# Two modulations' sums in another stage, and fewer steps and an earlier state in the state-space stage

## The chip, the cores and the metric

The kernel runs on one core of a Trainium2 chip. The metric is the device time of one execution in microseconds. The engines are TensorE (PE: matmuls; PEld: its weight loads), VectorE (DVE), ScalarE (ACT), GpSimd (POOL) and SyncE (SP), which issues nearly all transfers.

## The reference, cut to what matters

A block with attention and convolution and a gated feed-forward part come first; then a state-space mixer, then a mixer with stick-breaking attention. All in float32, 512 positions, width 1024.

```python
def swiglu_ffn(h, w_ffn_in, w_ffn_out):          # D_FF = 2816
    g, u = jnp.split(h @ w_ffn_in, 2, axis=-1)
    return (jax.nn.silu(g) * u) @ w_ffn_out

# state-space mixer: 32 heads of 64 in 4 groups, state of 128, chunks of 128 positions
z, xbc, dt = split(h @ in_w)
xbc = silu(causal_dwconv(xbc, conv_w, conv_b))   # -> xs, bm, cm
def step(state, inp):                            # one chunk
    acum = jnp.cumsum(ac, axis=1)
    seg = jnp.where(causal, acum[:, :, None] - acum[:, None, :], -jnp.inf)
    scores = einsum('btgn,bsgn->btsg', cc, bc)[..., None] * jnp.exp(seg)
    y_diag = einsum('btsgh,bsghp->btghp', scores, xc)
    y_off = einsum('btgn,bghpn->btghp', cc, state) * jnp.exp(acum)[..., None]
    new_state = state * jnp.exp(acum[:, -1]) + einsum('bsgn,bsghp->bghpn', bc, xc * w_end)
    return new_state, y_diag + y_off
y = (y + d_skip * xs) * silu(z);  y = group_rmsnorm(y) * norm_g;  x = x + gate * (y @ out_w)

# modulations: shift, scale, gate of each stage
shift, scale, gate = split(silu(c) @ ada_w[i] + ada_b[i], 3)     # ada_w[i]: 1024 x 3072
```

The modulation that the change speaks of is the shift and the scale of the last stage (`ada_w[1]`, columns 0 to 2047).

## The kernel before

**Products.** A float32 product is made of three matmuls: each operand is split in a high part (`fp32r`) and the rest. `mm3` issues high x high, L328, and the two mixed ones, L329 and L330. The stages run one after the other; each overlaps its edges with the next.

**Weights.** Each stage has a plan, a list of weight units of 512 KB in the order of their use. `load` (L247) brings a unit into one of four raw buffers (`NRAW`), `split` makes the high half `whi` on ACT (L269) and the low half `wlo` on DVE (L273), in a ring of four (`NRING`); PE frees a ring slot when it is done with the unit.

**Sums.** A modulation is a product of one row with a 1024 x 1024 matrix. It is not done on PE: eight loads of 512 KB go through the same raw buffers, and DVE adds each, times its scalar, to an accumulator `acc` (L503 the first, L505 the others). `add` puts the sums in the plan, `self.rate` of them after each weight unit. Sixteen steps after the eighth sum, `fin` adds up the partitions with 32 tiny matmuls (L487) and DVE turns the result into columns (L526 and L527 for a scale, such as `Gk`; L524 for a shift, such as `Sk`). While `summing` is set, the next modulation's first sum isn't started, and nothing behind it in the plan is:

```python
n = self.rate                                                # add()
self.plan += self.sums[:n]
if isinstance(u, Sums) and u.k == 0 and self.summing:        # advance()
    return False
```

**Steps.** The program text is a list of small steps. `run` merges lists by their share done (a list of 10 beside a list of 100 has one step for each ten) and after each step `pump` moves the plan on. The merged order, and a table of priorities by name (`PRIO`), give each instruction its place; a scheduler then fixes one order for each engine. Each engine executes its list in that order.

**Feed-forward stage** (about 320 to 650 us). `main` projects 256 columns of the gate and 256 of the other half in turn; ACT evicts the gate with SiLU (L1098), DVE multiplies (L1104) into `b` tiles. `Out` then projects back; its operands are split by L90 (ACT) and L91 (DVE).

**State-space stage** (about 690 to 1050 us). The input projection goes group by group; the projection of group g+1 (`main[g + 1]`) is merged with the steps `s` and `e` of `ssd(g)`; the last group is merged with the last z tiles (four products of 512 columns, evicted by ACT with SiLU, L1131) and the first output steps. In a group of eight heads:
- `scores`: four matmuls (L1234) and a copy on ACT (L1236). `bt`: transposes B (L1245), splits B (L1247) and C.
- `decay(i)`, for each of 8 heads: POOL masks (L1263), ACT takes four exponentials (L1266), DVE multiplies by the scores (L1268).
- `xs(c)`, for each of 4 chunks: PE transposes (L1275), DVE scales twice (L1277, L1278), POOL makes `xw` (L1282), ACT and POOL split it (L1239, L1240).
- `diag(c)`: 16 small matmuls (L1292); the first of a group waits for all eight decays. `state(c)`, c = 0 to 2: three matmuls, then a copy (L1315) or an addition on DVE (L1319), and the split again (L1239, L1240). `off(c)`, c = 1 to 3: three matmuls that read the split state of c-1.
- `e`: `gate`, `factor`, `norm` (L1338) and `trans` (L1344, copy L1345), which give the output projection's operand.

The accumulators in PSUM are of two kinds of four: `pa` for projections and `ps` for the rest.

Of the kernel before, what the change touches and what calls it, by code (L numbers as in the profile page):

```python
# [18 lines left out]
D = 1024  # L19
NT = S // P  # L20
# [109 lines left out]
class Body:  # L130
# [934 lines left out]
    def ffn(self):  # L1065
        nc, A = self.nc, self.A
        w = A["w_ffn_in"][0]
        a2, kw = A["ada_w_2"], A["kv_ada_w_2"]
        F = 2816
        g, gt, box = [], {}, {}  # L1070
        act = lambda: self.h

        def egt(t, ps):
            gt[t] = self.w512()
            nc.scalar.activation(gt[t], ps, AF.Silu)

        def eut(t, ps):
            nc.vector.tensor_tensor(gt[t], ps, gt[t], ALU.mult)
            pt = self.psum()
            for j in range(4):  # L1080
                nc.tensor.transpose(pt[:, j * P : (j + 1) * P], gt[t][:, j * P : (j + 1) * P], self.ident)
            nc.scalar.copy(g[0][:, :, t * P : (t + 1) * P], pt.rearrange("p (j c) -> p j c", j=4))


        self.first["ffn"] = self.proj_t(w, 0, act, egt, first=True)
        self.sums = (self.ada_row(A["ada_w"][0], 5 * D, A["ada_b"][:, 5 * D : 6 * D], A["ffn_post_g"], self.c1, "g2")
                     + self.ada_cols(a2[0], D, self.c2, "bGm", "gGm", "Gm")
                     + self.ada_cols(a2[0], 0, self.c2, "bSm", None, "Sm")
                     + self.ada_cols(kw, D, self.c2, "bGk", "gGk", "Gk")
                     + self.ada_cols(kw, 0, self.c2, "bSk", None, "Sk"))  # L1090
        ut = self.proj_t(w, F, act, eut)
        main = []
        for u0 in range(512, F, 256):
            gs = {}

            def eg(j, ps, gs=gs):
                gs[j] = self.w512()
                nc.scalar.activation(gs[j], ps, AF.Silu)  # L1098

            def eu(j, ps, gs=gs, u0=u0):  # L1100
                i = u0 // P + j
                if i // 4 == len(g):
                    g.append(self.big())
                nc.vector.tensor_tensor(g[i // 4][:, i % 4, :], ps, gs[j], ALU.mult)  # L1104

            main += self.proj_f(w, u0, 256, act, eg) + self.proj_f(w, F + u0, 256, act, eu)
        out = Out(self, A["w_ffn_out"][0], list(range(F // P)), lambda k: g[k // 4][:, k % 4, :])
        assert not self.sums
        yield
        self.stage = "ffn"  # L1110
        g.append(self.big())
        self.run(ut)
        self.run(main)
        self.run(out.rest(0))
        self.h = self.new_h()
        self.boundary(out, lambda: self.mods["g2"], True, ("Gm", "Sm"), act, self.first["mamba"])

    def mamba(self):
        nc, A = self.nc, self.A
# [33 lines left out]
        def pxbc(g):  # L1153
            return (self.proj_f(w, 4096 + g * P, P, act, conv(16 + g, lambda j: BC[0][:, 2 * (g % 2), :]))
                    + self.proj_f(w, 4608 + g * P, P, act, conv(20 + g, lambda j: BC[0][:, 2 * (g % 2) + 1, :]))
                    + self.proj_f(w, 2048 + g * 512, 512, act, conv(4 * g, dst(g))))
# [4 lines left out]
        def edt(ps):  # L1161
# [7 lines left out]

        pdt, dt1 = self.proj_32(w, 5120, act, lambda: self.dt_bias, edt)  # L1170
        a2 = A["ada_w_2"]
        self.sums = (self.ada_row(a2[0], 2 * D, A["ada_b_2"][0:1, 2 * D :], None, self.c2, "gm")
                     + self.ada_cols(a2[1], D, self.c2, "bGs", "gGs", "Gs")
                     + self.ada_cols(a2[1], 0, self.c2, "bSs", None, "Ss"))
        main = [pxbc(0)]
        for g in range(1, 4):
            main.append((self.proj_t(w, (g - 1) * 512, act, ez(g - 1)) if g > 1 else []) + pxbc(g))
# [45 lines left out]
        def ssd(g):  # L1223
# [121 lines left out]
                nc.scalar.copy(yT[g][:, :, cs_[c]], ps.rearrange("p (j c) -> p j c", j=4))  # L1345

            L = lambda f, *a: self.at(f.__name__, [lambda: f(*a)])[0]
            s = [L(rows, 0), L(rows, 1), L(scores), L(bt), L(xs, 0)] + [L(decay, i) for i in range(8)]
            s.insert(-2, L(state, 0))
            for c in range(NT):  # L1350
                if c + 1 < NT:
                    s += [L(xs, c + 1)]
                s += [L(diag, c)]
                if c > 0:
                    s += [L(off, c)]
                if 0 < c < NT - 1:
                    s += [L(state, c)]
            e = [L(gate, c) for c in range(NT)] + [L(factor), L(norm, 0)]
            for c in range(NT):
                e += ([L(norm, c + 1)] if c + 1 < NT else []) + [L(trans, c)]  # L1360
            return s, e
# [1 line left out]
        for g in range(3):  # L1363
            s, e = ssd(g)
            self.run(main[g + 1], s + e)
        s, e = ssd(3)
        self.run(main[4], s)
        self.run(out.steps((0, 1), range(4)), e)
# [357 lines left out]
```

## Time and profile before

| | |
|---|---|
| median of 3 runs | 1396.39 us (1393.24 to 1396.82) |
| profiled execution | 1390.66 us, span 1388.9 us |
| granted clock of TensorE, mean | 0.987 |
| PE busy | 1315.3 us (95%) |
| DVE, ACT, POOL busy | 885.8, 665.0, 313.8 us |

Busy time is a mean over stages with different limits; the state of one stage is read from a stretch of the trace. In a timeline's row the bracket is the time that the engine was idle before the instruction and what ended it. The time of the profiled execution lies 1.8 us over its span.

### The profile page before, as it was taken

How to read it: one execution, taken by the hardware profiler on the slowest of the kernel's cores; microseconds unless marked ns; L12 is line 12 of the kernel's file. 1: busy time of each engine (PE TensorE's matmuls, PEld its weight loads, DVE VectorE, ACT ScalarE, POOL GpSimd, SP SyncE). 2: the span in 40 equal slices, each digit the busy share in tenths (PEclk: the TensorE clock that was granted, in tenths of full speed). 3: DMA queues.
4: the chain of work that ended last, by engine and by line, in shares of the span. 5: the costliest groups of instructions: out<-in, count | busy, mean ns of one | idle time of the engine just before them, and what ended most of it. 6: DMA issues, size and time to landing. Idle time of an engine off the chain costs nothing. (4 is left out here: it accounts for less than half of the span.)

```text
span 1388.9 us, 19707 instructions
## 1 busy us (share of the span) xinstructions
PE 1315.3 (95%) x7477; PEld 1026.1 (74%) x7479; DVE 885.8 (64%) x1268; ACT 665.0 (48%) x1216; POOL 313.8 (23%) x321
## 2 busy tenths in 40 slices
PE   7799789999999999999999999999899999999997
PEld 5583566777888888888768777778688787777766
DVE  7844864466355443622768889767744966777865
ACT  5422375355222223412667566667542835555543
POOL 3441322014000000000111434342400412333421
PEclk9999989999999999999999999999999999999999
DMA  9679544205466655223157445424024354232311
GB/s 299 184 185 267 171 149 132 66 16 157 132 227 213 197 178 172 91 91 106 50 171 253 148 161 163 149 60 159 31 92 136 107 167 122 76 93 75 96 42 61
DMA packets 134731, 189.06 MB, mean 136 GB/s; under 512 B 10280, under 2 KB 95556, under 8 KB 133612
## 3 DMA queue, kind: packets, MB, share of 16 engines
q1 hardware_dynamic: 134588, 187.79, 44.3%
q8 instruction: 59, 0.97, 0.3%
q14 instruction: 36, 0.29, 0.1%
q10 hardware_dynamic: 48, 0.01, 0.0%
HBM read 178.25 MB, written 3.24 MB: 131 GB/s over the span
## 5 line engine op out<-in xcount | busy, mean ns | idle before, releaser
L273 DVE TENSOR_TENSOR wlo<-raw,whi 128x1024 fp32r<-128x1024 f32 (+1 forms) x161 | 212.9, 1334 | 202.9 <-ACT whi L269 192.8
L269 ACT CAST whi<-raw 128x1024 fp32r<-128x1024 f32 (+1 forms) x177 | 182.7, 1045 | 276.2 <-PE pa L329 116.1
L328 PE MATMUL pa<-b,whi 128*128 128x512 f32 x744 | 297.5, 400 | 0.0
L329 PE MATMUL pa<-b,whi 128*128 128x512 f32 x744 | 297.3, 400 | 0.0
L330 PE MATMUL pa<-b,wlo 128*128 128x512 f32 x744 | 296.1, 398 | 0.0
L505 DVE SCALAR_TENSOR_TENSOR acc<-raw,c,acc 128x1024 f32<-128x1024 f32 x84 | 122.4, 1457 | 74.5 <-DMA raw<-in_ada_w_dram 50.1
L328 PE MATMUL pa<-whi,b 128*128 128x512 f32 x424 | 165.9, 393 | 1.9 <-ACT b L90 1.5
L329 PE MATMUL pa<-wlo,b 128*128 128x512 f32 x424 | 166.1, 392 | 0.1
L330 PE MATMUL pa<-whi,b 128*128 128x512 f32 x424 | 165.8, 393 | 0.0
L328 PEld LDWEIGHTS pa<-b,whi 128*128 128x128 f32 x744 | 140.0, 188 | 32.5 <-issue 5.9
L330 PEld LDWEIGHTS pa<-b,wlo 128*128 128x128 f32 x744 | 140.1, 188 | 31.6 <-issue 1.7
L329 PEld LDWEIGHTS pa<-b,whi 128*128 128x128 f32 x744 | 140.0, 188 | 29.3 <-issue 0.5
L681 POOL TENSOR_TENSOR b<-w,b 128x512 fp32r<-128x512 f32 x24 | 36.9, 1555 | 461.6 <-DVE sm L586 288.1
L328 PEld LDWEIGHTS pa<-whi,b 128*128 128x128 f32 x424 | 79.8, 188 | 18.5 <-ACT b L90 1.6
L329 PEld LDWEIGHTS pa<-wlo,b 128*128 128x128 f32 x424 | 79.8, 188 | 17.2 <-DVE wlo L273 0.9
L330 PEld LDWEIGHTS pa<-whi,b 128*128 128x128 f32 x424 | 79.6, 188 | 17.2 <-issue 0.6
L1448 DVE TENSOR_TENSOR_SCAN w<-w,own 128x512 f32<-128x512 f32 (+3 forms) x64 | 64.1, 1047 | 15.2 <-ACT w L1445 15.2
L1450 POOL TENSOR_TENSOR w<-w,w 128x511 f32<-128x511 f32 (+3 forms) x64 | 67.8, 1064 | 22.1 <-DVE w L1448 21.2
L328 PE MATMUL ps<-whi,b 128*128 128x512 f32 x184 | 72.2, 393 | 0.0
L329 PE MATMUL ps<-wlo,b 128*128 128x512 f32 x184 | 72.1, 392 | 0.0
L330 PE MATMUL ps<-whi,b 128*128 128x512 f32 x184 | 71.9, 391 | 0.0
L777 PE MATMUL ps<-ident,w 128*128 128x128 f32 x240 | 55.0, 292 | 7.8 <-ACT w L787 4.0
(356 smaller groups left out, 2175.0 us busy)
## 6 DMA issues: line engine op xcount, KB each, us to landing
raw<-in_ada_w_dram SPq DMA_DIRECT2D x80, 512.0 KB
raw<-in_w_ffn_in_dram SPq DMA_DIRECT2D x44, 512.0 KB
raw<-in_m_in_w_dram SPq DMA_DIRECT2D x40, 512.0 KB
raw<-in_w_ffn_out_dram SPq DMA_DIRECT2D x22, 512.0 KB
b<-in_ada_w_dram SPq DMA_DIRECT2D x16, 512.0 KB
raw<-in_kv_ada_w_dram SPq DMA_DIRECT2D x16, 512.0 KB
b<-cumd SPq DMA_DIRECT2D x8, 1024.0 KB
raw<-in_m_out_w_dram SPq DMA_DIRECT2D x16, 512.0 KB
```

The lines of the kernel that those rows point to most:

```text
L269: nc.scalar.copy(hi[:, :n], u.raw)
L273: eng.tensor_tensor(lo[:, :n], u.raw, hi[:, :n].bitcast(F32), ALU.subtract)
L328: mm(ps, lhsT=lh, rhs=rh, start=first, stop=False)
L329: mm(ps, lhsT=lh, rhs=rl, start=False, stop=False)
L330: mm(ps, lhsT=ll, rhs=rh, start=False, stop=last)
L505: nc.vector.scalar_tensor_tensor(acc, raw, ck, acc, ALU.mult, ALU.add)
L681: nc.gpsimd.tensor_tensor(lo, y[i], hi.bitcast(F32), ALU.subtract)
L777: nc.tensor.transpose(ps[:, (t - s) * P : (t - s + 1) * P], Ps()[e][t][:, s * P : (s + 1) * P], self.ident)
L1448: nc.vector.tensor_tensor_scan(R[:, 0:N][:, ::-1], R[:, 0:N][:, ::-1], self.own[:, S - N : S][:, ::-1], 0.0, ALU.mult, ALU.max)
L1450: nc.gpsimd.tensor_tensor(pr_[:, : N - 1], pr_[:, : N - 1], R[:, 1:N], ALU.mult)
```

## The change

Three edits. The sums of `Gs` and `Ss`, scale and shift of the last stage, go from the plan of the state-space stage into that of the feed-forward stage, which has 56 sums instead of 40; there `rate` is 2 from column 2048 of the projection on, and 1 again for the output's units. In `ssd`, both `rows` and the `scores` are one step, the eight `decay` are two steps, and the four `gate` are two, so a group has 18 steps in `s` and 11 in `e` instead of 26 and 13. And `state(c)` stands in front of `diag(c)`; before, `state(0)` stood between the decays and `state(1)`, `state(2)` behind `off`.

```diff
+                     + self.ada_cols(kw, 0, self.c2, "bSk", None, "Sk")
+                     + self.ada_cols(a2[1], D, self.c2, "bGs", "gGs", "Gs")
+                     + self.ada_cols(a2[1], 0, self.c2, "bSs", None, "Ss"))
...
         for u0 in range(512, F, 256):
+            self.rate = 1 if u0 < 2048 else 2
...
+        self.rate = 1
         out = Out(self, A["w_ffn_out"][0], list(range(F // P)), lambda k: g[k // 4][:, k % 4, :])
...
-        self.sums = (self.ada_row(a2[0], 2 * D, A["ada_b_2"][0:1, 2 * D :], None, self.c2, "gm")
-                     + self.ada_cols(a2[1], D, self.c2, "bGs", "gGs", "Gs")
-                     + self.ada_cols(a2[1], 0, self.c2, "bSs", None, "Ss"))
+        self.sums = self.ada_row(a2[0], 2 * D, A["ada_b_2"][0:1, 2 * D :], None, self.c2, "gm")
...
-            s = [L(rows, 0), L(rows, 1), L(scores), L(bt), L(xs, 0)] + [L(decay, i) for i in range(8)]
-            s.insert(-2, L(state, 0))
+            both = lambda *fs: lambda: [f() for f in fs]
+            s = [both(L(rows, 0), L(rows, 1), L(scores)), L(bt), L(xs, 0)]
+            s += [both(*(L(decay, i) for i in range(4))), both(*(L(decay, i) for i in range(4, 8)))]
             for c in range(NT):
                 if c + 1 < NT:
-                    s += [L(xs, c + 1)]
+                    s += [L(xs, c + 1), L(state, c)]
                 s += [L(diag, c)]
                 if c > 0:
                     s += [L(off, c)]
-                if 0 < c < NT - 1:
-                    s += [L(state, c)]
-            e = [L(gate, c) for c in range(NT)] + [L(factor), L(norm, 0)]
+            e = [both(L(gate, 0), L(gate, 1)), both(L(gate, 2), L(gate, 3)), L(factor), L(norm, 0)]
```

The changed kernel's line numbers are higher by 2 in the state-space stage's `ssd` (L1266 is L1268, L1239 is L1241, L1236 is L1238), by 4 in its `ez` (L1131 is L1135) and by 3 in the feed-forward products (L1104 is L1107); the helpers' are the same.

ACT in group 1 of the state-space stage, behind the copy of the scores and the first eight exponentials (names with numbers; `b_6712` and `b_6950` are a tile of decays and the z tile). Before:

```order
L1247 CAST b_6748<-ps_6744 128x384
L1131 ACT_TABLE_LOAD
L1131 ACTIVATE b_6950<-pa_6705 128x512
L269 CAST whi_6925<-raw_6762 128x1024
L1239 CAST w_6779<-w_6777 128x512
L1131 ACTIVATE b_6950<-pa_6717 128x512
L1131 ACTIVATE b_6950<-pa_6726 128x512
L1131 ACTIVATE b_6950<-pa_6740 128x512
L1315 COPY w_6935<-ps_6931 128x512
L269 CAST whi_7004<-raw_6872 128x1024
L1239 CAST w_6936<-w_6935 128x512
L1266 ACT_TABLE_LOAD
```

In the changed order, from the last part of the first decay tile (`b_6808`) on to the end of the second (`b_6810`) and the z tile (`b_7064`):

```order
L1268 ACTIVATE b_6808<-b_6808,w_5975 128x128
L1317 COPY w_6995<-ps_6991 128x512
L1268 ACTIVATE b_6808<-b_6808,w_5975 128x128
L1241 CAST w_6996<-w_6995 128x512
L1268 ACTIVATE b_6808<-b_6808,w_5975 128x128 x3
L1268 ACTIVATE b_6810<-b_6810,w_5975 128x128 x7
L269 CAST whi_7116<-raw_6802 128x1024
L1268 ACTIVATE b_6810<-b_6810,w_5975 128x128 x9
L1135 ACT_TABLE_LOAD
L1135 ACTIVATE b_7064<-pa_6804 128x512
```

The four SiLU evictions of the z tile stood between the exponentials, with a table load on either side; now they stand behind the last exponential of the group, with one load.

DVE where the feed-forward products end and the output projection begins. Before, around the columns of `Sk` (`b_4671` to `b_4812` are operands of the output in halves; `wlo_4544` and `wlo_4564` are the low halves of its first two weight units, `wlo_4645` of the third):

```order
L273 TENSOR_TENSOR wlo_4544<-raw_4476,whi_4543 128x1024
L273 TENSOR_TENSOR wlo_4564<-raw_4482,whi_4563 128x1024
L524 TENSOR_TENSOR Sk<-ps_4573,bg 128x8
L1104 TENSOR_TENSOR b_4629<-pa_4569,w_4528 128x512
L91 TENSOR_TENSOR b_4671<-b_3065,b_4671 128x512 x2
L91 TENSOR_TENSOR b_4679<-b_3065,b_4679 128x512 x2
L91 TENSOR_TENSOR b_4747<-b_3324,b_4747 128x512
L273 TENSOR_TENSOR wlo_4645<-raw_4498,whi_4644 128x1024
L91 TENSOR_TENSOR b_4747<-b_3324,b_4747 128x512
L91 TENSOR_TENSOR b_4812<-b_3324,b_4812 128x512
L1104 TENSOR_TENSOR b_4629<-pa_4631,w_4561 128x512
```

In the changed order, from the third sum of the last modulation (`acc_4660` is the accumulator of `Ss`; the columns of `Gs`, L526, stand four rows ahead of the first row, followed by the first two sums) to the first low half of the output's weights, `wlo_4725`:

```order
L505 SCALAR_TENSOR_TENSOR acc_4660<-raw_4601,c_89,acc_4660 128x1024
L1107 TENSOR_TENSOR b_4685<-pa_4611,w_4570 128x512
L505 SCALAR_TENSOR_TENSOR acc_4660<-raw_4662,c_89,acc_4660 128x1024
L91 TENSOR_TENSOR b_4721<-b_3065,b_4721 128x512
L505 SCALAR_TENSOR_TENSOR acc_4660<-raw_4671,c_89,acc_4660 128x1024
L91 TENSOR_TENSOR b_4721<-b_3065,b_4721 128x512
L91 TENSOR_TENSOR b_4744<-b_3065,b_4744 128x512
L1107 TENSOR_TENSOR b_4685<-pa_4687,w_4609 128x512
L91 TENSOR_TENSOR b_4744<-b_3065,b_4744 128x512
L505 SCALAR_TENSOR_TENSOR acc_4660<-raw_4717,c_89,acc_4660 128x1024
L91 TENSOR_TENSOR b_4818<-b_3324,b_4818 128x512
L273 TENSOR_TENSOR wlo_4725<-raw_4665,whi_4724 128x1024
```

Sums now stand between the output's operand splits and ahead of the first low half, which moved from ahead of the last column sums to behind all but two of the last modulation's sums.

## Rows read from the trace of the kernel before

**Rows 1.** The page's list of engines; GB/s in 40 slices of the span.

```profile
PE 1315.3 (95%) x7477; PEld 1026.1 (74%) x7479; DVE 885.8 (64%) x1268; ACT 665.0 (48%) x1216; POOL 313.8 (23%) x321
...
GB/s 299 184 185 267 171 149 132 66 16 157 132 227 213 197 178 172 91 91 106 50 171 253 148 161 163 149 60 159 31 92 136 107 167 122 76 93 75 96 42 61
```

**Rows 2.** Table by stretch: us, PE PEld DVE ACT POOL busy, PEclk, DMA, GB/s.

```profile
400.00:640.00 240.00, 240.00 (x1301) 197.91 (x1300) 110.20 (x117) 65.79 (x81) 0.00 (x0) 1.00 0.50 161
690.00:1010.00 320.00, 299.80 (x1945) 237.08 (x1946) 251.84 (x372) 210.29 (x386) 109.00 (x98) 1.00 0.44 141
```

**Rows 3.** PE's waits, 690 to 1010 us: us in total, times, longest.

```profile
PE ps L329 <- POOL w L1240: 5.4, 8, 1.4
...
PE ps L328 <- ACT w L1239: 4.3, 6, 1.2
...
PE pa L328 <- ACT b L90: 1.5, 1, 1.5
...
PE ps L1292 <- DVE w L1277: 1.4, 1, 1.4
...
PE ps L1344 <- DVE b L1338: 1.3, 1, 1.3
```

**Rows 4.** PE's timeline, first diag of group 1: start, us, instruction.

```profile
845.66 0.39 PE L328 MATMUL pa<-b,whi 128*128 128x512 f32 x1
...
846.34 0.39 PE L328 MATMUL pa<-b,whi 128*128 128x512 f32 x1
...
847.65 1.15 PE L1292 MATMUL ps<-w,b 128*64 128x64 f32 x32 [0.93 <-issue]
```

**Rows 5.** PE's timeline at a state(0) and at an off(2).

```profile
830.75 0.50 PE L329 MATMUL ps<-w,b 128*128 128x512 f32 x1 [0.86 <-POOL w L1240]
...
857.58 0.73 PE L328 MATMUL ps<-w,b 128*128 128x512 f32 x2 [0.85 <-ACT w L1239]
```

**Rows 6.** ACT's timeline in group 1.

```profile
817.86 0.59 ACT L1236 COPY w<-ps 128x512 f32<-128x512 f32 x1
...
821.59 2.45 ACT L1266 ACTIVATE b<-b,w 128x128 f32<-128x128 f32 x8 [0.49 <-POOL b L1263]
...
825.64 1.28 ACT L1131 ACT_TABLE_LOAD   x1
...
826.93 0.60 ACT L1131 ACTIVATE b<-pa 128x512 f32<-128x512 f32 x1
```

**Rows 7.** DVE's timeline, the last decay of group 1.

```profile
846.86 0.69 DVE L1268 TENSOR_TENSOR b<-b,w 128x512 f32<-128x512 f32 x1
```

**Rows 8.** ACT's groups by shape, 690 to 1010: busy, mean ns, idle before.

```profile
L269 ACT CAST whi<-raw 128x1024 fp32r<-128x1024 f32 x41 | 42.8, 1044 | 14.3 <-PE pa L329 9.4 <-PE pa L330 4.7
...
L1266 ACT ACTIVATE b<-b,w 128x128 f32<-128x128 f32 x128 | 40.0, 390 | 1.0 <-POOL b L1263 0.9
...
L1239 ACT CAST w<-w 128x512 fp32r<-128x512 f32 x24 | 14.8, 618 | 38.1 <-POOL w L1282 23.7 <-DVE w L1319 14.3
...
L1131 ACT ACTIVATE b<-pa 128x512 f32<-128x512 f32 x16 | 9.0, 600 | 4.2 <-PE pa L330 4.1
```

**Rows 9.** POOL's low halves: minimum, median and maximum in ns.

```profile
L1240 POOL TENSOR_TENSOR w<-w,w x24: 1269/1297/2167, 770.8 to 996.7; 128x512 fp32r<-128x512 f32 x24
```

**Rows 10.** DVE's timeline in the feed-forward stage.

```profile
484.42 1.29 DVE L505 SCALAR_TENSOR_TENSOR acc<-raw,c,acc 128x1024 f32<-128x1024 f32 x1 [1.30 <-DMA raw<-in_kv_ada_w_dram]
...
556.90 3.09 DVE L91 TENSOR_TENSOR b<-b,b 128x512 fp32r<-128x512 f32 x5
...
559.90 1.22 DVE L273 TENSOR_TENSOR wlo<-raw,whi 128x1024 fp32r<-128x1024 f32 x1
```

**Rows 11.** SP's queue, the issue of the sum's load at 484.42.

```profile
480.60 0.33 SPq L247 DMA_DIRECT2D raw<-in_kv_ada_w_dram  x1
```

**Rows 12.** ACT's waits, 390 to 640 us.

```profile
ACT whi L269 <- PE pa L329: 80.6, 26, 7.5
...
ACT whi L269 <- DMA raw<-in_w_ffn_in_dram: 11.7, 5, 4.1
```

More of the change, by code (lines that the diff above doesn't have):

```diff
@@ L1089, in ffn @@
                      + self.ada_cols(kw, D, self.c2, "bGk", "gGk", "Gk")
-                     + self.ada_cols(kw, 0, self.c2, "bSk", None, "Sk"))
+                     + self.ada_cols(kw, 0, self.c2, "bSk", None, "Sk")
+                     + self.ada_cols(a2[1], D, self.c2, "bGs", "gGs", "Gs")
+                     + self.ada_cols(a2[1], 0, self.c2, "bSs", None, "Ss"))
         ut = self.proj_t(w, F, act, eut)
```

## The prediction

> **What bounds the kernel now.** I read the page's list of engines first: TensorE (PE) is busy 95% of the span [rows 1]. The table by stretch then splits that [rows 2]. Over 240 us of the feed-forward stage PE never stops and DVE is busy 110 of 240; over 320 us of the state-space stage PE is busy 299.80, so 20 us is all that the second part of the change can win there, and DVE (252) and ACT (210) are nearly as loaded. PE's table of waits for that stretch names the losers [rows 3]; the timeline of PE gives the beat, three 512-column matmuls from 845.66 to 846.34, so 0.227 us each [rows 4], and the places [rows 5]. So the stage is bound by PE with holes where a short chain of casts on ACT, POOL and DVE isn't done in time, and the feed-forward stage by PE alone, with spare time on the others.
>
> By place the waits are: state(0), 7 waits, about 5.5 us, mostly in the row on POOL's low half, with two of the casts in ACT's row (0.41, 0.56); off(2) and off(3), 4.3 us (0.85 twice, 1.25, 0.40 on ACT's high half, 0.18 and 0.80 on POOL's low half); diag(0) 0.93 and 0.4; and in the last group, which has no projection of another group beside it, 4.2 us in diag(3), the output's first split and the first transposition (1.4, 1.5, 1.3) [rows 3].
>
> **The state ahead of the diagonal products.** off(c+1) needs state(c) through a DVE addition, an ACT cast (0.62, [rows 8]) and a POOL subtraction (median 1.30, [rows 9]). Before, PE had 2.8 to 4.4 us of matmuls between the end of state(1) and off(2), and waited on top; in the changed order, counting matmuls at 0.227, it has 6.1 to 14.9, and 5.8 to 9.9 before off(3) where it had 3.3 to 4.2. A chain that took about 5.2 (4.4 and 0.85 of wait) fits in 6.1. All off waits go: -4.3. Nothing else is late there at once, but state(2) now stands so close behind its own xs that its xw (a POOL product, a cast, a subtraction) has 3.2 us in group 0 and 2.25 in group 3, against about 4.5 needed: new waits of 1.3 and 2, **+3.2** (bounds 0 and 5). state(0) keeps 2.2 to 3.4 us for that same chain, so its waits stay: I take +1.2 for the two places where the distance shrinks (bounds -1.5 and +3).
>
> **Fewer steps.** With 29 steps for 39 the same instructions are spread over the same projection, and the scores come later in it. What is queued behind is ACT's list: 32 exponentials, then DVE's product, which diag(0) waits for. In group 1 this ran from the scores' copy at 817.86 to the end of DVE's last product at 847.55, 29.7 us [rows 6, 7], and PE, with 26.3 us of matmuls and small waits, was 0.93 late [rows 4]. The changed order of ACT (first pair of order rows) drops from that list two table loads (2.57, at 1283 ns, [rows 6]), four SiLU evictions at 0.56 (2.25; 9.0 us for 16) and two weight casts (2.09 at 1.044, [rows 8]), and takes in one copy (0.56): 23.4 us. PE's own list from the scores to diag(0) falls from 26.3 to 14.1 us, to which come 2.5 of state(0)'s waits and 1.8 of small ones: 18.4. So PE stops 5.0 us, **+4.1** over before. It has nothing else to do then: the four z tiles that the projection has finished hold all four accumulators until ACT evicts them behind the exponentials. Bounds: if the 32 exponentials run at 0.31 rather than at their mean of 0.39 [rows 8], as a run of eight did (2.45 us from 821.59, [rows 6]), the wait is 2.5; at 0.39 and with POOL's masks behind, 6.5. In the other groups PE keeps 17.8 to 20.2 us and the wait stays nothing to 0.4. In the last group the shorter list of steps leaves diag(3), the output's split and the transposition time: -3.9 (bounds -4.2 and 0).
>
> The Trainium skill ("ScalarE: Activation LUTs", section "What ACT_TABLE_LOAD costs") says that a table switch costs 1283 ns and a drain of about 1380 more. The row agrees with the first and not with the second: the load at 825.64 takes 1.28 and the next activation begins at 826.93 [rows 6]. By the page ACT would lose four loads' 10.6 us in the stage in place of 5.1, and group 1's list would end 2.8 us earlier, its wait near 2.
>
> State-space stage: -4.3 + 3.2 + 1.2 + 4.1 - 3.9 = **+0.3**. The 16 sums that leave (16 x 1.28 = 20.6 us of DVE, [rows 10]) are worth nothing by themselves where no wait of PE is on DVE's list; the waits on DVE are the last group's, where no sum stood.
>
> **The sums in the feed-forward stage.** They add 16 loads of 512 KB and 16 DVE instructions of 1.28 us [rows 10]. DVE has room in the mean (110 + 20.6 of 240, [rows 2]) and the lead of the weight ring covers a late load in most places: ACT itself waits 26 times, 80.6 us, for PE to free a ring slot [rows 12]. Two places have no cover.
>
> First, the rate. From column 2048 on, each weight unit (24 matmuls, 5.44 us) brings two sums, so three loads of 524288 B in 5.44 us, 289 GB/s where the stretch now has 161 [rows 2]. The fastest of the page's 40 slices moved 299 [rows 1], so the loads fit with nothing to spare; I count **+1.2** for one or two late weight units (bounds 0 and 9).
>
> Second, the seam to the output projection. A modulation's first sum can't start before the column sums of the one before are done, so the eight sums of the last shift, Ss, stand behind Gs on DVE, and DVE runs in order. Before, the low halves of the output's first two weight units stood ahead of the last column sums, Sk, and behind Sk came one product, five splits and the third unit's low half (second pair of order rows; the five took 3.09, [rows 10]). Now stand there: the two small ones of Gs (0.3), one first sum (0.75), five sums at 1.28 with queueing 1.3, two products and five splits at 0.6 and the low half at 1.22: 13.0 us. On PE, from Gs's column sums to the first matmul that reads that low half, are 44 matmuls, 10.0 us. So PE waits at least 3.0, and 3.5 with the landing of one of those sums, which come 3.8 us after issue [rows 10, 11]: **+3.3** (bounds 2 and 6). Sum of the stage +4.5.
>
> What else is moved: the same 16 loads leave SP's queue in the state-space stage, where DMA engines are 44% busy [rows 2]; no load there is waited for by PE, so nothing.
>
> **The sum.** +0.3 + 4.5 = +4.8 us on the profiled execution's 1390.66, so 1395.5. That run lies 0.41% under the median of the runs shown, 1396.39; scaled, **1401 us**.
>
> **Rivals.**
> *Loads saturate* (slower). If two sums a unit don't come at 289 GB/s but at some 270, twelve units at 5.82 us for 5.44 end 4.6 us late, and the burst in front of the seam adds to the 3.3 since sums still to land hold DVE: 12 to 13 us in the feed-forward stage, **1409**. For it: 161 GB/s in the mean hides bursts, and 5 of ACT's casts already wait on loads, 11.7 us [rows 12]. Against: the ring's four slots, up to 20 us of lead, absorb 4.6 us.
>
> *Chains shorten too* (the other side). DVE without sums in the state-space stage starts each xdt, state addition and low half earlier, so that xw, and with it state(0) and state(2), are ready; ACT's list of group 1 ends by PE's 18.4 us. Then nothing replaces the 4.3 and 3.9, state(0)'s waits shrink by some 1.5, and only the seam's 3.3 stands against it: -6.4, **1390**. It decides where group 1's list is under 19 us. For it: DVE's 252 of 320 busy falls by 20 [rows 2], and four table loads go. Against: the exponentials and casts alone come to 18 us, and state(0)'s waits name POOL. The Trainium skill speaks for it: "SBUF — State Buffer", section "SBUF: two separate sides", has POOL blocked for a whole instruction by a DVE operation that reads two SBUF operands, as a sum does. The trace agrees for single cases only: POOL's subtraction took 1269 ns at least and 2167 at most, but 1297 in the median [rows 9], so few met one. By the rule alone the gain is below 1 us.
>
> *No change.* Half of group 1's wait (2.5) and the seam at its lower end (2.5) with nothing at the rate: -1.3 + 2.5 = +1, **1398**. For it: the order of the instructions shows neither that exponentials may run ahead of the scores nor how far they pipeline. This is also the case in which the step counts do nothing but exchange one wait for another.
>
> **How the numbers follow.** Two medians of this kernel can be told apart from about 0.3%, 4.2 us: faster is under 1392.2, slower over 1400.6. The forecast has 0.42 (own range 1397 to 1405, so 0.26 of it slower and 0.16 the same), saturated loads 0.16, shorter chains 0.22, no change 0.20. So faster 0.22, same 0.36, slower 0.42. The range takes in the centres of all four: 1388 to 1410.
>
> **What would show it.** PE's waits of off on ACT's high half gone, and a wait of 2.5 to 6.5 us on the first diag of group 1 with ACT's exponentials or DVE's product behind it; PE waits of 1 to 2 us at state(2) of the first and last group; a PE wait of 2 to 6 us at the first low-half matmuls of the output projection, with DVE's sums ahead of that low half; the feed-forward stretch longer by 3 to 6 us. I am wrong if PE stays without waits in the feed-forward stage, if diag(0) of group 1 waits under 1 us, or if weight casts there wait for their loads for more than 15 us in all.

## The result, and the profile after

The changed kernel takes 1403.75 us (median of 6 runs, 1400.58 to 1405.01) against 1396.61 (6 runs, 1393.24 to 1397.27): the ratio is 1.0055, with a 95% interval of 1.0042 to 1.0068. It is slower by 7.1 us; 1401 had been forecast, in a range of 1388 to 1410. The profiled execution took 1403.58 us, with a span of 1401.8. Medians here and below are of fast runs; one run of 6823 us, of the kernel with state(1) alone ahead, is left out.

Three marks on PE cut a span into stretches that can be compared: the first column sums of the feed-forward stage (L487) and the first transposition of the boundary behind each stage (L664). PE's timeline has them, for the kernel before:

```profile
423.36 0.30 PE L487 MATMUL ps<-ones,acc 128*32 128x1 f32 x16
...
675.78 0.38 PE L664 MATMUL pa<-ident,w 128*128 128x128 f32 x2
...
1079.65 0.38 PE L664 MATMUL pa<-ident,w 128*128 128x128 f32 x2
```

and for the changed one:

```profile
429.07 0.29 PE L487 MATMUL ps<-ones,acc 128*32 128x1 f32 x14
...
688.49 0.27 PE L664 MATMUL pa<-ident,w 128*128 128x128 f32 x1
...
1093.45 0.39 PE L664 MATMUL pa<-ident,w 128*128 128x128 f32 x2
```

From the first mark to the second the feed-forward stage takes 252.4 us before and 259.4 after, +7.0. From the second to the third the state-space stage takes 403.9 and 405.0, +1.1. Ahead of the first mark the two kernels have the same instructions in the same order; that the first mark is 5.7 us later is a difference between two executions, not between the kernels. Over the eleven executions that follow it lies between 422.7 and 430.8.

The seam to the output projection is the new loss. DVE's timeline from the columns of `Gs` (L526) to the output's first low half:

```profile
560.71 0.16 DVE L526 SCALAR_TENSOR_TENSOR Gs<-ps,bg 128x8 f32<-128x8 f32 x1
...
561.57 2.61 DVE L505 SCALAR_TENSOR_TENSOR acc<-raw,c,acc 128x1024 f32<-128x1024 f32 x2
...
567.92 1.28 DVE L505 SCALAR_TENSOR_TENSOR acc<-raw,c,acc 128x1024 f32<-128x1024 f32 x1 [1.35 <-DMA raw<-in_ada_w_dram]
...
571.52 1.28 DVE L505 SCALAR_TENSOR_TENSOR acc<-raw,c,acc 128x1024 f32<-128x1024 f32 x1
572.72 0.69 DVE L91 TENSOR_TENSOR b<-b,b 128x512 fp32r<-128x512 f32 x1
573.32 1.22 DVE L273 TENSOR_TENSOR wlo<-raw,whi 128x1024 fp32r<-128x1024 f32 x1
```

That is 13.8 us from 560.71 to 574.54 on DVE (13.0 were counted), one late load among them. PE's timeline in the same place:

```profile
571.06 0.50 PE L328 MATMUL pa<-whi,b 128*128 128x512 f32 x1 [1.06 <-DVE b L1107]
...
574.60 0.79 PE L329 MATMUL pa<-wlo,b 128*128 128x512 f32 x1 [2.57 <-DVE wlo L273]
575.19 0.63 PE L330 MATMUL pa<-whi,b 128*128 128x512 f32 x1
...
577.32 0.45 PE L329 MATMUL pa<-wlo,b 128*128 128x512 f32 x1
577.61 0.39 PE L330 MATMUL pa<-whi,b 128*128 128x512 f32 x1
```

PE waits 1.06 and 2.57 us where nothing waited before [rows 2], and the seven matmuls from 574.60 to 577.61 come 0.43 us apart in the mean, where 0.227 is the beat [rows 4]. The granted clock of these 3 us is 0.53, so PE ran at the lower of the two clock levels nearly all the time: another 1.4 us lost.

PE's waits in the state-space stage (us, times, longest), against [rows 3]:

```profile
PE ps L329 <- POOL w L1242: 5.3, 8, 1.1
PE ps L1294 <- issue: 4.3, 1, 4.3
...
PE ps L328 <- ACT w L1241: 3.5, 4, 1.5
...
PE ps L1294 <- DVE b L1270: 1.7, 2, 1.1
PE ps L1346 <- DVE b L1340: 1.7, 1, 1.7
PE ps L328 <- ACT b L1249: 1.1, 1, 1.1
...
PE ps L1294 <- DVE w L1321: 0.7, 1, 0.7
```

The totals of the cast rows look like those of before (5.4 + 4.3, and 0.4 on L1247, make 10.1 then; 5.3 + 3.5, and 1.1 on L1249, make 9.9 now), but their places have changed: the off waits are down to 0.8 and the states have the rest. The wait of 4.3 us is the first diag of group 1, which took 0.93 before [rows 4].

### The profile page after: what moved, and what is told of

Read it like the earlier page. It is cut to its first block, busy times and chain, and to the rows that moved or that the text cites. A ratio compares the mean times of both kernels' runs of the same rounds, so it can differ in the third digit from the quotient of the medians.

```text
span 1401.8 us, 19727 instructions
## 1 busy us (share of the span) xinstructions
PE 1322.0 (94%) x7477; PEld 1029.0 (73%) x7479; DVE 881.0 (63%) x1268; ACT 659.5 (47%) x1212; POOL 311.8 (22%) x321
## 5 line engine op out<-in xcount | busy, mean ns | idle before, releaser
L505 DVE SCALAR_TENSOR_TENSOR acc<-raw,c,acc 128x1024 f32<-128x1024 f32 x84 | 119.0, 1417 | 66.0 <-DMA raw<-in_ada_w_dram 54.5
L1452 POOL TENSOR_TENSOR w<-w,w 128x511 f32<-128x511 f32 (+3 forms) x64 | 67.7, 1062 | 22.1 <-DVE w L1450 21.2
```

Source lines behind the costliest of these rows:

```text
L505: nc.vector.scalar_tensor_tensor(acc, raw, ck, acc, ALU.mult, ALU.add)
L1452: nc.gpsimd.tensor_tensor(pr_[:, : N - 1], pr_[:, : N - 1], R[:, 1:N], ALU.mult)
```

## The experiments

Each kernel below is the kernel before with the edit shown, or the changed kernel where that is said. "Seam stretch" is the one from the first to the second mark, "state-space" from the second to the third, each from the one profiled execution; "PE idle" is the part of the state-space stretch in which PE was not busy. The eight combinations of the three edits are gathered here:

| sums moved | steps merged | state ahead | seam stretch | state-space | PE idle | time against before |
|---|---|---|---|---|---|---|
| no | no | no | 252.4 | 403.9 | 22.0 | 1 |
| yes | no | no | 260.1, 260.8 | 403.6, 401.8 | 19.5, 19.4 | 1.0017 (1.0003 to 1.0031) |
| no | yes | no | 252.3 | 413.8 | 25.5 | 1.0054 (1.0034 to 1.0074) |
| no | no | yes | 252.4 | 423.3 | 30.9 | 1.0104 (1.0086 to 1.0122) |
| no | yes | yes | 252.4 | 423.6 | 35.0 | 1.0123 (1.0095 to 1.0152) |
| yes | yes | no | 259.3 | 407.1 | 20.3 | 1.0058 (1.0037 to 1.0079) |
| yes | no | yes | 256.8 | 409.2 | 26.3 | 1.0076 (1.0053 to 1.0099) |
| yes | yes | yes | 259.4 | 405.0 | 23.1 | 1.0055 (1.0042 to 1.0068) |

The idle time is not the whole loss. The state-space stretch before, with only the sums moved, and with only the state ahead (columns as in [rows 2]):

```profile
675.80:1079.60 403.80, 381.83 (x2313) 303.83 (x2312) 295.99 (x450) 246.41 (x455) 112.77 (x100) 1.00 0.42 132
686.70:1090.30 403.60, 384.14 (x2249) 303.66 (x2248) 276.33 (x432) 246.48 (x454) 114.48 (x100) 0.99 0.35 112
676.70:1099.90 423.20, 392.28 (x2313) 309.72 (x2312) 299.23 (x453) 244.72 (x454) 114.26 (x100) 0.97 0.39 126
```

With the state ahead, 9 of the 19.4 us are idle time. In the other 10.5 PE is busy longer with as many matmuls, at a mean granted clock of 0.97 where it was 1.00: the lower level, which the forecasts below give no price.

**Only the sums moved.**

```diff
+                     + self.ada_cols(a2[1], D, self.c2, "bGs", "gGs", "Gs")
+                     + self.ada_cols(a2[1], 0, self.c2, "bSs", None, "Ss"))
...
+            self.rate = 1 if u0 < 2048 else 2
```

> Only the sums move; the state-space steps are those of before. My theory (the loss is a few placed waits of PE): the wait at the seam to the output projection stays, because DVE's order there is the same as in the changed kernel; PE waits 3 to 5 us at the output's first low halves, the feed-forward stage is 4.5 to 6 us longer than before, the state-space stage keeps its off waits (about 4) and has no wait over 2 us at a first diag; time 1400 to 1403. Rival (the sums are harmless and the loss is all in the state-space stage): 1396 to 1398. Rival (the transfers saturate): over 5 us of waits on weight loads in the stretch with two sums per unit, and 1405 or more.

Measured: 1397.66 us against 1395.49, ratio 1.0017 (1.0003 to 1.0031). PE's waits in the feed-forward stretch on the low half and on L1107 are there, 2.6 and 1.4 us, and the stretch is 7.7 longer; the state-space stage is as long as before. So the place and the size of the seam are as I held, but the time, 2.2 us more, is under my 1400 and fits the first rival's number. A cost of 7 us in the trace and of 0.4 to 4.3 in the times do not agree; the profiled execution was the slowest of ten.

**The same kernel once more, for its trace.**

> The kernel with only the sums moved, once more, for its trace: its first profiled execution was the slowest of ten and 4.7 us over their median. If the seam's cost is fixed by the order of instructions, the stretch from the first column sums of the feed-forward stage to its end takes 259 to 261 us again (252.4 without the sums). If it varies with how the transfers land, 254 to 258.

Measured: 260.8 us in the stretch, so the first cost was no accident. But the order alone does not fix it: the three other kernels with the same order up to the second mark took 259.3, 259.4 and 256.8 (table). The wait on the low half is alike in all (2.6 to 2.8 us); the wait on the product is 1.0 to 1.4 and, in the 256.8, none, and PE ran at the lower clock level behind them for 5 us here and not at all in the 256.8 (last section). This execution took 1397.41 us; its state-space stage, 401.8, is 2.1 shorter than before, which gives part of it back. In both traces of this kernel PE idles less in that stage (19.5 and 19.4 us for 22.0), so the sums that leave take some 2.5 us of waits out of it. More lies ahead of the first mark, where the one trace of before is among the fastest (423.4, and 425.7 in the mean of the other twelve). How much of the 7 us the sums alone cost in the mean is left between 2 and 6.

**Both state-space edits, the sums where they were.** The whole of the diff's last part, and nothing else:

```diff
+            s = [both(L(rows, 0), L(rows, 1), L(scores)), L(bt), L(xs, 0)]
...
+                    s += [L(xs, c + 1), L(state, c)]
```

> Only the steps and the earlier state; the sums stay in the state-space stage. My theory: the feed-forward stage is as before; in group 1 PE has 11.2 us of matmuls between scores and the first diag (14.1 in the changed kernel, 26.3 before) and waits 5 to 9 us there; the off waits are gone except about 1 us in group 0; time 1399 to 1404. Rival (the gain of the state-space edits is real and the sums alone cost the time): 1388 to 1394.

Measured: 1412.27 us, ratio 1.0123 (1.0095 to 1.0152), more than I had expected. Its PE waits:

```profile
PE ps L1292 <- DVE b L1268: 9.6, 1, 9.6
PE ps L329 <- POOL w L1240: 8.4, 9, 4.9
PE ps L1344 <- DVE b L1338: 3.9, 3, 2.0
```

The stage takes 423.6 us with the sums in it and 405.0 without: moving the sums is worth 18.6 us to the edited stage, 11.9 of them PE's idle time, and little in length (403.9; 403.6 and 401.8) to the old one.

**Only the state ahead.** The diff's line with `L(state, c)`, in the list of 39 steps.

> Only the state ahead of the diagonal products, with the 39 steps of before. My theory: the waits change places. The off waits fall from 4.3 to under 1.5 us, but state(2) stands 2.0 to 2.7 us behind its xs in all four groups and waits about 2 us in each, so state waits grow by 5 to 8; the first diag of group 1 waits about 2; time 1398 to 1403. Rival (the earlier state is a pure gain of the 4.3 us): 1390 to 1393.

Measured: 1410.17 us, ratio 1.0104 (1.0086 to 1.0122), 7 over my range. The off waits fell as expected, but the two largest waits, 7.2 and 3.1 us, are first diags, of the last group and of group 1:

```profile
PE ps L1292 <- issue: 8.7, 2, 7.2
PE ps L329 <- POOL w L1240: 7.3, 12, 1.4
...
PE ps L1292 <- DVE b L1268: 3.1, 1, 3.1
```

A state that stands earlier pushes the scores of the next groups later. In the last group 13.0 us of matmuls lay between scores and first diag, where the kernel before has 22.1 (counted in the order); I had that number and left it out of the sum.

**Only the steps merged.**

```diff
+            s = [both(L(rows, 0), L(rows, 1), L(scores)), L(bt), L(xs, 0)]
+            s += [both(*(L(decay, i) for i in range(4))), L(state, 0), both(*(L(decay, i) for i in range(4, 8)))]
...
+            e = [both(L(gate, 0), L(gate, 1)), both(L(gate, 2), L(gate, 3)), L(factor), L(norm, 0)]
```

> Only the steps merged (rows and scores in one, decays in two, gates in two), the state where it was (state(0) between the two halves of the decays). My theory: group 1's first diag waits 5 to 9 us (10.7 us of matmuls between scores and diag, an exponential chain of about 23), the last group's end gains about 3, off waits stay at 2 to 4; time 1399 to 1404. Rival (fewer steps cost nothing): 1392 to 1397.

Measured: 1402.64 us, as expected; group 1's first diag waits

```profile
842.97 0.38 PE L1292 MATMUL ps<-w,b 128*64 128x64 f32 x2 [7.56 <-DVE b L1268]
```

**The sums moved, the state ahead** (39 steps).

> The sums moved and the state ahead, with the 39 steps of before. Theory (the state-space edits cost what they do because DVE's sums run beside short chains; without the sums the waits of state(0) and state(2) are all that is left): the state-space stage takes 403 to 409 us, 15 to 20 less than with the sums in it (423.3); time 1400 to 1406. Rival (the sums in the stage don't matter, as they don't for the steps of before, 403.9 with and 403.6 without): 418 or more, and 1412 or more in all.

Measured: 1406.24 us, ratio 1.0076 (1.0053 to 1.0099); the stage 409.2, 14.1 less than with the sums in it. The length is at the edge of my range, but not for my reason: the largest wait left is no state's but the first diag's in the last group (11.4 us of matmuls between scores and first diag):

```profile
989.31 0.48 PE L1294 MATMUL ps<-w,b 128*64 128x64 f32 x4 [9.53 <-issue]
```

**The sums moved, the steps merged.**

> The sums moved and the steps merged, with the state where it was. Theory as for the run before: the state-space stage takes 403 to 408 us (413.8 with the sums in it), with a wait of 3 to 6 us at group 1's first diag (15.0 us of matmuls between scores and diag); time 1400 to 1405. Rival: 412 or more, and 1408 or more.

Measured: 1401.82 us, the stage 407.1, group 1's first diag:

```profile
846.06 1.02 PE L1294 MATMUL ps<-w,b 128*64 128x64 f32 x14 [3.82 <-issue]
```

So the 4.3 us of the changed kernel in group 1 belong to the merged steps (3.8 with them, none with the old steps and the sums gone), and the merged steps spare the last group the 9.5 of the earlier state.

**What the sums do to the stage.** Both state-space edits with sums and loads in place, but 14 of the 16 sums add 8 of 1024 columns.

```diff
+                    n = 8 if thin else D
+                    nc.vector.scalar_tensor_tensor(acc[:, :n], raw[:, :n], ck, acc[:, :n], ALU.mult, ALU.add)
```

> Both state-space edits with the sums still in that stage, their 16 loads too, but 14 of the 16 sums add 8 of their 1024 columns only (so the last stage's modulation is left out in most columns). Theory A (DVE's 18 us of sums, and POOL waiting beside them, lengthen the chains): the state-space stage falls from 423.6 to 404 to 409 us, the wait at group 1's first diag from 9.6 to 4 to 6. Theory B (the loads, the ring of raw buffers and the place of the sums in the plan do it): 418 or more, the wait stays near 9.

Measured: 1397.41 us, ratio 1.0013 (1.0000 to 1.0027). The stage falls from 423.6 to 410.4, the wait at group 1's first diag from 9.60 to 7.93, and PE's waits on POOL's low halves from 8.4 to 3.8, nearly all of it one wait of 4.91. Neither theory's number was met; 13 of the 18.6 us go with DVE's work on the sums. Of the 5.4 that are left, PE is busy longer for 3.9 (385.8 us for 381.9, a set of column sums among it); what the loads and the places of the sums in the plan cost is not shown. Where the 9.6 came from is seen in the timelines of DVE and POOL of the kernel with both edits and full sums, ahead of the decays of group 1:

```profile
840.35 3.20 DVE L505 SCALAR_TENSOR_TENSOR acc<-raw,c,acc 128x1024 f32<-128x1024 f32 x2
848.30 1.57 DVE L1268 TENSOR_TENSOR b<-b,w 128x512 f32<-128x512 f32 x1 [4.75 <-DMA raw<-in_m_in_w_dram]
...
838.10 4.37 POOL L1263 TENSOR_SCALAR_AFFINE_SELECT b<-b 128x512 f32<-128x512 f32 x4
842.45 2.23 POOL L1240 TENSOR_TENSOR w<-w,w 128x512 fp32r<-128x512 f32 x1
```

The first decay's product starts 4.75 us after the sums end (the name in the bracket is not its operand; ACT's exponentials stood still too, behind a cast that waited 4.85 for POOL's xw). POOL made that xw behind four masks and a low half that ran in part beside the two sums and took 4.37 and 2.23 us; the four masks before took 2.85, and a low half takes 1.30 in the median [rows 9]. One late link stops three engines that execute in order.

**Two sums per unit from column 1536** (the changed kernel):

```diff
-            self.rate = 1 if u0 < 2048 else 2
+            self.rate = 1 if u0 < 1536 else 2
```

> The changed kernel with two sums per unit from column 1536 on instead of 2048, so that the last modulation's sums are done before the output projection's weight units. Theory of the seam (sums queued on DVE ahead of the output's first low halves cost the feed-forward stage): its 385.6 us fall to 380 to 382, PE has no wait on a low half at the output's start, time 1397 to 1400. Rival (the transfers of a stretch with two sums per unit cost it, or the throttled clock does): the stretch is longer, 20 units for 12, the stage stays at 385 or more, time 1403 or more.

Measured: 1401.3 us, ratio 1.0043 (1.0028 to 1.0059). The seam's waits are gone, but in the stretch with two sums per unit there are six new ones:

```profile
PE pa L328 <- ACT whi L269: 1.4, 3, 0.8
PE pa L330 <- DVE wlo L273: 0.9, 3, 0.3
```

2.3 us there for 3.6 at the seam: the stretch is 258.3 us, 1.1 less than in the changed kernel and 5.9 over before. The stage that I had at 385.6 is 384.4: the waits moved as the theory of the seam has it, but the gain did not come. Both theories had a part.

**State(1) alone ahead of its diag**, an attempt to keep the gain:

```diff
+            s += [L(xs, 1), L(diag, 0), L(xs, 2), L(state, 1), L(diag, 1), L(off, 1), L(xs, 3), L(diag, 2), L(off, 2), L(state, 2), L(diag, 3), L(off, 3)]
```

> The kernel before with one edit: state(1) alone stands ahead of diag(1), in all four groups; state(0), state(2), the steps and the sums stay. Theory (a state gains PE time where it moves away from its off and loses it where it moves close behind its own xs; state(1) has 11 to 14 us behind its xs, so it only gains): the off waits fall from about 4 to under 2 and the state waits stay; against it, the last group has 16.4 us of matmuls between scores and first diag where it had 22.1, a wait of 0 to 5. State-space stage 399 to 404 us, time 1390 to 1396. Rival (any state ahead of its diag costs time, as the run with all three did): stage over 408, time over 1400.

Measured: 1404.87 us (median of five runs), ratio 1.0084 (1.0057 to 1.0111), the stage 415.0. My theory fell. The off waits did not even shrink, since off(2) came only 0.5 us later behind state(1) in the order, and the last group's first diag waits:

```profile
PE ps L329 <- POOL w L1240: 7.5, 11, 1.4
PE ps L1292 <- issue: 6.2, 2, 4.8
PE ps L328 <- ACT w L1239: 5.4, 6, 1.2
```

**The same in group 0 alone.**

```diff
+            early = g == 0
...
+                if c == 1 and early:
+                    s += [L(state, 1)]
```

> The same edit in the first group alone; the order of the other groups stays as before to the instruction. Theory: the two off waits of group 0 (0.85 and 0.18 in the trace of before) go, nothing else changes: 1 to 1.5 us less in that group, 1392 to 1395 in all, which cannot be told from no change by the time and only by the trace. Rival (the waits come back later in the group): group 0 as long as before.

Measured: 1397.63 us against 1393.44, ratio 1.0029 (1.0011 to 1.0047): the rival, and worse. From scores to scores group 0 takes 68.0 us for 63.1. The two off waits stayed (0.98 and 0.17), a third one, of 1.12 us, came, and the wait for DVE's convolution is 1.74 where it was 0.40; PE is also busy 1.9 us longer, at a granted clock of 0.97. Which of DVE's instructions held that convolution was not followed up.

No version beat the kernel before.

## Why the prediction was right

The direction, the time and the two places were right. The time alone says little: the range took in the centres of all four cases, no change among them. The sum of +4.8 stands against 8.1 in the traces (+0.3 for 1.1 in the state-space stage, +4.5 for 7.0 in the feed-forward stage) and 7.1 in the medians. Point by point:

- *off waits, -4.3*: right. They fell to about 0.8, -3.5; the largest left is in group 0:

```profile
808.20 0.51 PE L329 MATMUL ps<-w,b 128*128 128x512 f32 x1 [0.63 <-POOL w L1242]
```

- *state(0) +1.2, state(2) +3.2*: right in the mechanism. The waits that the two rows of casts keep are at state(0) of all four groups, +1.6, and at state(2) of the first and last group, +2.0, the largest:

```profile
797.95 0.50 PE L329 MATMUL ps<-w,b 128*128 128x512 f32 x1 [1.12 <-POOL w L1242]
```

- *Group 1's first diag, 5.0*: 4.33 measured, the right place and nearly the right size. ACT's copy of the scores at 828.26 and the last product's end at 850.48 are 22.2 us apart (23.4 counted):

```profile
828.26 0.59 ACT L1238 COPY w<-ps 128x512 f32<-128x512 f32 x1 [0.71 <-PE ps L1236]
...
848.79 1.28 ACT L1135 ACT_TABLE_LOAD   x1
850.08 1.08 ACT L1135 ACTIVATE b<-pa 128x512 f32<-128x512 f32 x2
...
847.98 2.50 DVE L1270 TENSOR_TENSOR b<-b,w 128x512 f32<-128x512 f32 x4 [0.59 <-ACT b L1268]
...
849.38 1.98 PE L1294 MATMUL ps<-w,b 128*64 128x64 f32 x32 [4.33 <-issue]
...
849.30:853.30 4.00, 3.92 (x56) 3.40 (x58) 2.56 (x4) 3.22 (x6) 0.00 (x0) 0.50 0.29 107
```

  The first diag did not wait for all eight products here, as the list of the stage's parts has it: it starts at 849.38, and the last product, from 849.80 on, is still to come. And the sum has no term for the clock: behind the wait it was granted at 0.50 (the last row, columns as in [rows 2]), and the first diag took 1.98 us for 1.15 [rows 4].

  The z tile's first eviction (850.08) begins right behind the table load, as in [rows 6], so the drain that the Trainium skill ("ScalarE: Activation LUTs", section "What ACT_TABLE_LOAD costs") adds to it does not show here either, and the estimate by the row, not by the page, was the nearer one.
- *Last group's end, -3.9*: half right. The output's first split no longer waits, diag(3) waits 0.7 for 1.4, but the first transposition 1.7 for 1.3: -1.8. A first diag of 1.1 us in group 2 was not foreseen.
- *The seam, +3.3*: 3.6 measured, with the wait on the product that I hadn't named. Mis-sized is the whole feed-forward term, +4.5 for 7.0: left out were the matmuls at the lower clock after the wait (1.4), the column sums of `Gs`, 0.7 us of PE, that moved in from the other stage (those of `Ss`, at 691.63, fall behind the second mark), and about 1 us in steps of 0.1 to 0.2 over the beat around the waits. The rate term, +1.2, was 0.3 in this kernel; with 20 such units the waits came to 2.3.
- *The sums that leave are worth nothing to the state-space stage*: wrong. In the old order the stage's length hardly changes, but PE idles 2.5 us less; for the edited one they are worth 18.6 us. The sum came near because it was worked from the changed order, whose lists had no sums in them; as a statement on the parts it was wrong, since it took them to be additive.
- *Rivals*: late loads do show, and with them one of the three signs of being wrong: read of the feed-forward stretch, ACT's weight casts wait 32.2 us in all for their loads, where 15 was the limit and 2.0 is the time before.

```profile
ACT whi L269 <- DMA raw<-in_w_ffn_in_dram: 32.2, 8, 6.0
```

  The ring's lead covers them: PE loses 0.3 us to it here and 2.3 in the kernel with 20 units, and not 9; whether short transfers or late issues hold the loads, no run tells apart. The shorter chains of the other side do show, at 18.6 us, but only against the other edits' longer ones. The Trainium skill's rule on the port that DVE and POOL share ("SBUF — State Buffer", section "SBUF: two separate sides") fits the one place where POOL's instructions took longer beside two sums (4.37 and 2.23 us, above), which is most of the fall of PE's waits from 8.4 to 3.8 without the sums' work. It is not the rule of the stage: the median of POOL's low halves is 1.30 us with the sums and 1.29 without their work. That it is this port and nothing else that held POOL there, no run shows.

## What to carry to other kernels

Edits to one pipelined stage are not additive: the same two edits cost the stage 19.7 us beside the sums and 1.4 to 3.2 without them, so price a combination from its own order of instructions. When a chain is moved ahead of what needs it, count the distance to what it needs as well, in every group, and the distances of the groups behind it. A wait of TensorE can cost more than its length, where the lower clock level follows it: 10.5 of 19.4 us with the state ahead. Work that is moved into idle time of an in-order engine costs where it queues ahead of a short deadline, here one seam, and not by its share of the engine.

## What was not expected of the hardware

After a wait PE can run at the lower level for some microseconds. In the kernel with both state-space edits a wait of 4.91 us was followed by matmuls 0.43 us apart up to 850.01, and the stretch behind it, which holds the wait of 9.6, was granted 0.61 of full speed (columns as in [rows 2]):

```profile
844.73 0.80 PE L329 MATMUL ps<-w,b 128*128 128x512 f32 x1 [4.91 <-POOL w L1240]
845.32 0.63 PE L330 MATMUL ps<-w,b 128*128 128x512 f32 x1
```

```profile
845.00:860.00 15.00, 5.98 (x15) 4.39 (x15) 8.96 (x11) 11.46 (x30) 3.23 (x3) 0.61 0.38 110
```

It does not follow each time: in the kernel with the sums moved and the state ahead, the seam's wait of 2.82 us was followed by the full beat; in the second trace of the kernel with only the sums moved one of 2.56 was followed by twelve matmuls 0.43 us apart. What decides between them is not shown.

```profile
568.34 0.50 PE L329 MATMUL pa<-wlo,b 128*128 128x512 f32 x1 [2.82 <-DVE wlo L273]
568.67 0.39 PE L330 MATMUL pa<-whi,b 128*128 128x512 f32 x1
```
